# A streaming LoRA kernel on one core: a 16-tile load cut into two of 8 tiles, stores that follow, and the last wait moved to GpSimd

## The chip, the cores and the metric

The kernel runs on one core of one Trainium2 chip. The metric is the device time of one execution in microseconds (us); the time of a kernel is the median of its runs. A profile is a further execution of the same program, recorded by the hardware profiler. Its span runs from the first to the last instruction of the core; the execution's own time lies a little above its span.

## The reference, cut to what matters

```python
batch, seq, d_model, r = 16, 512, 768, 16
# x: [16, 512, 768], A: [768, 16], B: [16, 768], scale = 0.5, all float32
lora = np.matmul(np.matmul(x, A), B)
return (x + scale * lora).astype(np.float32)
```

With the two outer dimensions of x flattened there are 8192 rows of 768 numbers. Each row is read once (25.2 MB in all), gets a correction of rank 16 and is written once (another 25.2 MB).

## The kernel before

**Tiles and pieces.** The 8192 rows are 64 tiles of 128 rows. All of x stays on the chip in one buffer, `xs`, with 64 slots per partition; results are added in place and stored from the same buffer, so no load ever waits for a buffer to come free. The tiles come in seven loads, `LOADS = [2, 2, 4, 8, 16, 16, 16]` (line 13), and leave in nine stores, `STORES = [2, 2, 4, 8, 16, 8, 8, 8, 8]` (line 14). One load covers a contiguous stretch of rows of x, and each partition takes `n` consecutive rows of it (`rows`, a `"(p s) d -> p s d"` view), so a load of 16 tiles moves one run of 16 x 3072 bytes for each of 128 partitions, and a load of 8 tiles one run of 8 x 3072 bytes. A store takes a slice of the load's piece that its tiles belong to.

**Chunks.** Arithmetic goes by chunks of four tiles, 16 chunks in all (`CHUNK = 4`). For one chunk:

- VectorE (line 94, two casts) and ScalarE (line 92, one cast) narrow x to float16 in `xh`. The first cast of each engine that touches a new load waits for that load (`narrowed`).
- TensorE transposes the narrowed blocks by matmuls with an identity (line 185), ScalarE copies the transposes out of PSUM (line 135), TensorE multiplies them by A (line 193), and ScalarE copies that result, scaled, to `yt` (line 139).
- TensorE multiplies `yt` by B (line 204, one tile at a time into two PSUM buffers), and VectorE adds the product to x in place (line 146, `summed`).

**Order.** Each engine's order is written out by hand, and engines wait for each other through semaphores alone. On VectorE the casts of chunk c+1 stand between the additions of chunk c-1: cast, two additions, cast, two additions (the loop that calls `narrowed` and `summed`). So a cast that waits for a load holds up the additions behind it. TensorE works on chunk c while it expands chunk c-1. After the last addition that a store needs, VectorE drains (line 150) and raises the semaphore `added`.

**Queues.** All loads and stores are issued by SyncE (lines 81, 110, 113 and 124), in this order: two loads, A, B, the other loads but the last, a wait for `prep` (A and B have been taken out of the slots that they borrow in `xs`), the last load, and then for each store a wait on `added` and the store. Every store raises the one semaphore `stored` by 16 when it has landed. SyncE's last instruction waits until all of them have.

**GpSimd** has little to do: it zeroes the borrowed slots and builds the identity at the start (lines 98 to 101), and then runs straight to the end of the program.

Of the kernel before, what the change touches and what calls it, by code (L numbers as in the profile page):

```python
# [9 lines left out]
MM_DT = mybir.dt.float16  # L10


LOADS = [2, 2, 4, 8, 16, 16, 16]
STORES = [2, 2, 4, 8, 16, 8, 8, 8, 8]

CHUNK = 4

# [2 lines left out]
def kernel(  # L20
# [8 lines left out]
    nc = tc.nc  # L29
# [14 lines left out]
    NB = D // 32  # L44
    assert D % W == 0 and sum(LOADS) == NT == sum(STORES)
    n_splits = [(n0, min(512, D - n0)) for n0 in range(0, D, 512)]
# [16 lines left out]

    room = NT - LOADS[-1]
    a_rows = xs[0:32, room, 0 : 32 * R].rearrange("b (a r) -> b a r", r=R)
# [3 lines left out]
    def rows(t2, t0, n):  # L69
        return t2[ds(t0 * P, n * P), :].rearrange("(p s) d -> p s d", s=n)  # L70

    with tc.tile_critical():  # L72
        names = "zeroed ident a b a_t prep fed0 fed1 fed2 turned got proj y lora freed added".split()
        S = {k: nc.alloc_semaphore(name=f"s_{k}") for k in names}
        landed = [nc.alloc_semaphore(name=f"s_load{i}") for i in range(len(LOADS))]
        stored = nc.alloc_semaphore(name="s_stored")
        part_of = [i for i, n in enumerate(LOADS) for _ in range(n)]

        def load(i):
            t0, n = sum(LOADS[:i]), LOADS[i]  # L80
            nc.sync.dma_start(out=xs[:, t0 : t0 + n, :], in_=rows(x2, t0, n)).then_inc(landed[i], 16)
# [31 lines left out]
        nc.sync.dma_start(out=b_f32, in_=B).then_inc(S["b"], 16)  # L113
        for i in range(2, len(LOADS) - 1):
            load(i)
        nc.sync.wait_ge(S["prep"], 1)
        load(len(LOADS) - 1)
        done = 0
        for k, n in enumerate(STORES):
            i = part_of[done]  # L120
# [4 lines left out]
                out=rows(out2, t0, w)[:, piece, :], in_=xs[:, done : done + n, :]  # L125
            ).then_inc(stored, 16)
            done += n
        nc.sync.wait_ge(stored, 16 * len(STORES))


        narrowed(nc.scalar, 0, 2)
# [19 lines left out]

        ends = {sum(STORES[: i + 1]) for i in range(len(STORES))}
        nc.vector.sem_inc(S["freed"], 2)
# [112 lines left out]
```

## Time and profile before

| what | before |
|---|---|
| median of three runs | 128.37 us |
| the three runs | 126.47, 128.37, 132.39 us |
| the profiled execution's own time | 126.03 us |
| span of the profiled execution | 124.3 us |
| mean granted TensorE clock | 0.855 |
| bytes moved by DMA | 50.45 MB, mean 406 GB/s |
| busy: TensorE, VectorE, ScalarE, GpSimd | 93.0, 80.2, 76.7, 1.2 us |

A view that gives a table by stretches has, for each stretch of time, its length, the busy time of each engine with the number of instructions that started in it, the granted TensorE clock, the mean busy share of the 16 DMA engines and the rate in GB/s. A packet counts where it starts, so that in short stretches the share can be over 1. A view of waits says which engine and line stood idle, for whom, how long in total, how often, and the longest. In a timeline a row has its start, its length, the engine, the line, the operation and, in square brackets, the idle time before it and what ended that.

### The profile page before, as it was taken

How to read it: one execution, taken by the hardware profiler on the slowest of the kernel's cores; microseconds unless marked ns; L12 is line 12 of the kernel's file. 1: busy time of each engine (PE TensorE's matmuls, PEld its weight loads, DVE VectorE, ACT ScalarE, POOL GpSimd, SP SyncE). 2: the span in 40 equal slices, each digit the busy share in tenths (PEclk: the TensorE clock that was granted, in tenths of full speed). 3: DMA queues.
4: the chain of work that ended last, by engine and by line, in shares of the span. 5: the costliest groups of instructions: out<-in, count | busy, mean ns of one | idle time of the engine just before them, and what ended most of it. 6: DMA issues, size and time to landing. Idle time of an engine off the chain costs nothing. (4 is left out here: it accounts for less than half of the span.)

```text
span 124.3 us, 1800 instructions
## 1 busy us (share of the span) xinstructions
PE 93.0 (75%) x608; PEld 42.0 (34%) x608; DVE 80.2 (65%) x102; ACT 76.7 (62%) x129; POOL 1.2 (1%) x7
## 2 busy tenths in 40 slices
PE   0014996999259999999999999999999999750000
PEld 0012443345115335425544445444454445210000
DVE  0049208993195744655999999989999997773000
ACT  0047498688516266347989889898898988600000
POOL 3000000000000000000000000000000000000000
PEclk9999999999955555557999999999999999995555
DMA  3999999799699979969799999998989999998980
GB/s 89 406 399 435 459 522 443 316 506 475 301 491 506 443 316 506 477 301 491 309 414 443 459 435 475 475 443 348 491 348 443 435 403 467 403 451 340 388 380 8
DMA packets 2374, 50.45 MB, mean 406 GB/s; under 512 B 284, under 2 KB 284, under 8 KB 836
## 3 DMA queue, kind: packets, MB, share of 16 engines
q1 hardware_dynamic: 2372, 50.43, 95.5%
q14 instruction: 2, 0.02, 0.0%
HBM read 25.26 MB, written 25.17 MB: 406 GB/s over the span
## 5 line engine op out<-in xcount | busy, mean ns | idle before, releaser
L146 DVE TENSOR_TENSOR xs<-xs,lo_ps 128x768 f32<-128x768 f32 x64 | 58.1, 950 | 10.0 <-PE lo_ps L204 9.7
L135 ACT CAST xt<-xt_ps 128x512 f16<-128x512 f32 x96 | 52.5, 579 | 14.4 <-PE xt_ps L185 12.9
L185 PE MATMUL xt_ps<-ident,xh 128*128 128x128 f16 x384 | 37.0, 240 | 8.8 <-PEq L178 8.8
L193 PE MATMUL yt_ps<-xt,a_mm 128*16 128x512 f16 x96 | 35.8, 431 | 1.6 <-PEq L178 1.6
L94 DVE CAST xh<-xs 128x1024 f16<-128x1024 f32 x32 | 22.0, 690 | 22.6 <-DMA xs<-in_x_dram 18.0
L204 PE MATMUL lo_ps<-b_mm,yt 16*128 16x512 f16 (+1 forms) x128 | 29.9, 352 | 8.4 <-PEq L178 6.6
L185 PEld LDWEIGHTS xt_ps<-ident,xh 128*128 128x128 f16 x384 | 24.8, 107 | 29.4 <-issue 29.4
L92 ACT CAST xh<-xs 128x1024 f16<-128x1024 f32 x16 | 16.8, 1047 | 1.2 <-DMA xs<-in_x_dram 1.2
L204 PEld LDWEIGHTS lo_ps<-b_mm,yt 16*128 16x128 f16 x128 | 9.9, 96 | 20.0 <-issue 15.3
L139 ACT ACTIVATE yt<-yt_ps 16x512 f16<-16x512 f32 x16 | 9.4, 587 | 8.3 <-PE yt_ps L193 8.3
L193 PEld LDWEIGHTS yt_ps<-xt,a_mm 128*16 128x16 f16 x96 | 7.3, 89 | 20.1 <-issue 15.9
L92 ACT ACT_TABLE_LOAD x1 | 1.3, 1283 | 8.0 <-DMA xs<-in_x_dram 8.0
L158 DVE STREAM_TRANSPOSE xs<-xs 32x512 f32<-32x512 f32 x1 | 1.0, 1036 | 0.0
L162 DVE CAST a_mm<-xs 32x96 f16<-32x96 f32 x4 | 0.9, 232 | 0.1
L164 DVE CAST b_mm<-xs 16x768 f16<-16x768 f32 x1 | 0.5, 547 | 0.0
L98 POOL MEMSET xs<- 32x512 f32 x1 | 0.5, 514 | 0.5 <-SPq L72 0.5
L101 POOL TENSOR_SCALAR_AFFINE_SELECT ident<-ident 128x128 f16<-128x128 f16 x1 | 0.3, 292 | 0.2 <-POOL ident L99 0.2
L99 POOL MEMSET ident<- 128x128 f16 x1 | 0.2, 194 | 0.0
L247 POOL MEMSET const-bfloat16-1.0<- 128x1 bf16 x1 | 0.1, 102 | 0.0
L247 POOL MEMSET const-uint8-127<- 128x1 uint8 x1 | 0.1, 102 | 0.0
L247 POOL MEMSET const-float32-0.0<- 128x1 f32 x1 | 0.1, 99 | 0.2 <-issue 0.2
L247 POOL MEMSET const-float32-1.0<- 128x1 f32 x1 | 0.1, 99 | 0.0
## 6 DMA issues: line engine op xcount, KB each, us to landing
xs<-in_x_dram SPq DMA_DIRECT2D x3, 6144.0 KB, 43.7
out_dram<-xs SPq DMA_DIRECT2D x5, 3072.0 KB, 15.0
out_dram<-xs SPq DMA_DIRECT2D x1, 6144.0 KB, 20.2
xs<-in_x_dram SPq DMA_DIRECT2D x1, 3072.0 KB, 15.7
xs<-in_x_dram SPq DMA_DIRECT2D x2, 768.0 KB, 5.5
xs<-in_x_dram SPq DMA_DIRECT2D x1, 1536.0 KB, 8.9
out_dram<-xs SPq DMA_DIRECT2D x2, 768.0 KB, 42.8
out_dram<-xs SPq DMA_DIRECT2D x1, 1536.0 KB, 41.2
```

Source lines behind the costliest of these rows:

```text
L92: i = engine.copy(out=xh[u], in_=src)
L94: i = engine.tensor_copy(out=xh[u], in_=src)
L98: nc.gpsimd.memset(a_rows, 0.0).then_inc(S["zeroed"], 1)
L135: nc.scalar.copy(out=xt[j], in_=xt_ps[j % NX]).then_inc(S["got"], 1)
L139: nc.scalar.activation(out=yt, in_=yt_ps, func=mybir.ActivationFunctionType.Copy, scale=sc).then_inc(S["y"], 1)
L146: nc.vector.tensor_tensor(out=xs[:, k, :], in0=xs[:, k, :], in1=lo_ps[k % 2], op=add).then_inc(S["freed"], 1)
L158: nc.vector.transpose(out=a_t, in_=a_rows.rearrange("b a r -> b r a")).then_inc(S["a_t"], 1)
L162: nc.vector.tensor_copy(out=a_mm[ds(32 * k, 32), :, :], in_=a_tv[:, k, :, :])
L164: nc.vector.tensor_copy(out=b_mm, in_=b_f32).then_inc(S["prep"], 1)
L185: i = nc.tensor.matmul(xt_ps[j % NX][:, ds(s * P, P)], xh[u][:, s, ds(h * P, P)], ident, start=True, stop=True,)
L193: i = nc.tensor.matmul(yt_ps, a_mm[:, j, :], xt[j], start=(j == 0), stop=(j == ND - 1))
L204: i = nc.tensor.matmul(lo_ps[s % 2][:, ds(n0, w)], yt[:, ds(s * P, P)], b_mm[:, ds(n0, w)], start=True, stop=True,)
```

## The change

The load of tiles 16 to 31 becomes two loads of 8 tiles, so that there are eight loads. The store of tiles 16 to 31 becomes two stores of 8 tiles, one for each of these pieces, so that there are ten stores of at most 8 tiles. The wait for all stores moves from SyncE's queue to GpSimd's, where it comes after the building of the identity. The arithmetic and its order on TensorE, VectorE and ScalarE stay as they are; VectorE gets one more drain and semaphore, and its wait for tiles 16 to 31 becomes two waits, one for each piece.

```diff
-LOADS = [2, 2, 4, 8, 16, 16, 16]
-STORES = [2, 2, 4, 8, 16, 8, 8, 8, 8]
+LOADS = [2, 2, 4, 8, 8, 8, 16, 16]
+STORES = [2, 2, 4, 8, 8, 8, 8, 8, 8, 8]
...
             ).then_inc(stored, 16)
             done += n
-        nc.sync.wait_ge(stored, 16 * len(STORES))
+
+        nc.gpsimd.wait_ge(stored, 16 * len(STORES))
```

## The prediction, made before the changed kernel was run

> **What bounds the kernel now.** I read the page's slices first (DMA at 9 nearly throughout, the clock at 5 for a stretch in the middle and at the end), then the waits, then tables by stretches around both places, then each DMA's time to landing. The page's slices:
>
> ```profile
> PEclk9999999999955555557999999999999999995555
> DMA  3999999799699979969799999998989999998980
> ```
>
> A kernel that moves 50.45 MB with its DMA engines at work from 3 to 122 us is bound by transfers unless these run dry. They run dry once, as this table by stretches shows:
>
> ```profile
> 111.00:112.00 1.00, 0.48 (x2) 0.12 (x2) 1.00 (x3) 0.00 (x0) 0.00 (x0) 1.00 0.97 418
> 112.00:112.80 0.80, 0.00 (x0) 0.00 (x0) 0.80 (x2) 0.00 (x0) 0.00 (x0) 0.63 0.43 184
> 112.80:113.40 0.60, 0.00 (x0) 0.00 (x0) 0.12 (x1) 0.00 (x0) 0.00 (x0) 0.50 0.10 41
> 113.40:114.20 0.80, 0.00 (x0) 0.00 (x0) 0.00 (x0) 0.00 (x0) 0.00 (x0) 0.50 1.08 461
> 114.20:121.30 7.10, 0.00 (x0) 0.00 (x0) 0.00 (x0) 0.00 (x0) 0.00 (x0) 0.50 0.92 391
> 121.30:122.30 1.00, 0.00 (x0) 0.00 (x0) 0.00 (x0) 0.00 (x0) 0.00 (x0) 0.50 0.06 25
> ```
>
> The share falls to 0.43 and 0.10 while VectorE makes the last addition, that is 0.8 x 0.57 + 0.6 x 0.90 = 1.0 us lost, and recovers when the last store arrives. At the end a share of 0.06, one engine of 16, is still working 1 us after the rest. So two things end together: VectorE hands over the last store 1.0 us late for 15 DMA engines, and one DMA engine lags, never runs dry and sets the end. The landing views say how it came to lag: the last four stores, of 8 tiles each, issued at 83.1, 93.4, 103.6 and 113.0, took 17.6, 15.0, 12.1 and 10.0, so they landed at 100.7, 108.4, 115.7 and 123.0. The steps are 7.7, 7.3 and 7.3 (and 7.7 before them: the store of 72.8 took 20.2). Loads show the undisturbed pace: the loads of tiles 16 to 31 and 32 to 47 landed at 3.86 + 29.7 = 33.55 and 48.1, 14.5 for 16 tiles or 7.27 for 8. While the engines compute, the laggard loses 0.4 us per 8-tile store; when they stop, nothing.
>
> Why is VectorE so late? The waits, and the timeline at the longest of them that has a load behind it in mid-stream:
>
> ```profile
> DVE xh L94 <- DMA xs<-in_x_dram: 18.0, 3, 8.0
> DVE xs L146 <- PE lo_ps L204: 9.7, 16, 2.2
> ```
>
> ```profile
> 33.64 0.69 DVE L94 CAST xh<-xs 128x1024 f16<-128x1024 f32 x1 [4.66 <-DMA xs<-in_x_dram]
> ```
>
> The first of VectorE's three waits, 8.0, is the start; the second, 5.4 at 19.1, is for tiles 8 to 15; the third, 4.66, is for the 16-tile load, and is the one that the change touches. TensorE starves with it, and its clock goes:
>
> ```profile
> 29.00:31.80 2.80, 2.73 (x19) 1.24 (x19) 0.00 (x0) 2.36 (x5) 0.00 (x0) 1.00 0.81 351
> 31.80:35.30 3.50, 0.00 (x0) 0.00 (x0) 1.66 (x3) 1.63 (x2) 0.00 (x0) 0.77 1.04 449
> 35.30:57.60 22.30, 22.19 (x97) 8.95 (x98) 13.65 (x17) 11.30 (x20) 0.00 (x0) 0.50 0.98 424
> 57.60:112.20 54.60, 50.82 (x376) 23.68 (x374) 49.47 (x61) 44.84 (x77) 0.00 (x0) 1.00 1.01 429
> ```
>
> TensorE does nothing from 31.8 to 35.3, the clock is halved within that stretch, and for the next 22.3 us TensorE is busy 22.19 and yet shows only 97 matmuls, 4.3 a us against 376 / 54.6 = 6.9 afterwards. VectorE's first casts of chunks 4 and 8 stand at 33.64 and 62.32, 28.7 us for four chunks. From chunk 8 to chunk 15 (98.35) it is 36.0 for seven, 5.15 each. The half clock therefore cost 28.7 - 4 x 5.15 = 8.1 us of compute.
>
> **The change part by part.**
>
> *The load cut in two.* Tiles 16 to 23 land one half-load after tiles 8 to 15 (3.3 + 15.7 = 19.0, plus 7.27), at 26.3; tiles 24 to 31 at 33.6 as now. VectorE comes to the cast of chunk 4 at 33.64 - 4.66 = 28.98, 2.7 after the landing, so the 4.66 goes. What is late next: at 5.15 a chunk it wants tiles 24 to 31 (chunk 6) at 39.3, against 33.6; tiles 32 to 47 (chunk 8) at 49.6, against 48.1 and about 0.1 for the cut; tiles 48 to 63 (chunk 12) at 70.2, against 11.8 + 51.0 = 62.8. The thinnest cover is 1.4 us at chunk 8; if it is gone, VectorE waits what is missing and has room for it (below). Without the idle stretch at 31.8 the clock should stay, so chunk 15 comes at 28.98 + 11 x 5.15 = 85.6 instead of 98.35, and the last addition ends at 113.0 - 12.7 = 100.3.
>
> *The stores.* With adds two chunks behind the casts, the stores of tiles 16-23, 24-31 and so on issue near 49.5, 59.8, 70.1, 80.4, 90.7 and 100.3. The queue needs each of them when the one before has landed: 77.5 for the first (the store issued at 47.0 took 30.5), then one every 7.27: 84.8, 92.0, 99.3, 106.6 and 113.8. An engine without the lag needs them up to 1 us earlier. The cover is 12 us or more, and 4 even if the clock falls as it does now (8.1 us). So the hole of 1.0 us closes. This is worth nothing by itself, since the laggard never saw the hole. The laggard gains where compute stops 12.7 us earlier: 12.7 / 7.7 x 0.4 = 0.65 us. Bounds: nothing, if its lag comes from the stores themselves; and at most its whole distance to the others without the hole, 1.3 (122.95 against about 121.6) + 1.0 = 2.3. I take 0.65, as the two steps of 7.3 are the row nearest to it.
>
> *More transfers.* One more load and one more store. The load of tiles 8 to 15 took 19.0 - 11.7 = 7.3 from the landing before it (2.82 + 8.9), twice that is 14.6, against 14.5 for 16 tiles at once: 0.07 for a load, the same taken for a store, +0.1 in all; the low bound is 0, the high bound 0.4 (two of the steps of 7.7 against 7.3). SP issues one DMA more ahead of its wait for `prep` (0.45 us a DMA): it now waits 7.0 us there, which hides it, and the last load would otherwise start up to 0.5 later against 51.0 in the queue.
>
> The Trainium skill, "DMA: Bandwidth & Descriptors", sections "Anatomy of one DMA" and "Rules for kernel authors", speaks against the cut: a transfer has a fixed cost of about 2 us, fitted on the GpSimd path, and many small ones should be joined into a large one. By it two more transfers in a full queue would add up to 4 us; the rows above, one landing straight behind another, say 0.1.
>
> *One more drain on VectorE*, with what it stands ahead of, the next cast. The nine drains last 1.5 us in the median but overlap the addition that they wait for; even all of it lies under the 12 of cover. 0.
>
> *The last wait on GpSimd.* Behind it on GpSimd is only the end of the program; its own work ended at 2.1 us. SP, which now waits 9.6 us there, passes on and meets the others at the end barrier, all of which then wait for GpSimd. From the landing, 122.95, to the span's end lie 1.3 us. GpSimd's wait for its own memset at the start cost it 0.23, SP's waits at the barrier 0.5 to 0.7: I take 0, from -0.3 (a hop less) to +0.5 (a hop more).
>
> *Sum*, against the profiled execution: 126.03 - 0.65 + 0.1 + 0 = **125.5 us**. Bounds: 126.03 - 2.3 - 0.3 = 123.4, and 126.03 + 0.4 + 0.5 = 126.9. This execution is 2.3 below the median shown (128.37) and 0.4 below the lowest run. Why the runs spread over 126.5 to 132.4 no row shows. The profiled one has no slack at all between VectorE and the last store, so each us that the clock stays low longer goes to the end; this is my reading of the spread, and the change would take it away with 12 us of slack. So 125.5 stands for the median too, -2.2%.
>
> The trace has 22.3 us at half clock with TensorE busy for 22.19 of them. The Trainium skill, "TensorE: Matmul & The Clock Gate", section "The HAM clock gate", lets the full clock return after about 3.4 us of sustained work. By the page the half clock would have cost an estimated 1.7 us (half of 3.4) and not 8.1, so the change would bring VectorE's end forward by 4.66 + 1.7 = 6.4 only, to 106.6 instead of 100.3; by either the last store is issued ahead of the queue, and the sum is the same but for some 0.3 of the laggard's gain.
>
> **The rivals.**
>
> 1. *The spread is the transfers' own* (some runs move bytes more slowly). For it: DMA is near 9 in all slices, and the one lagging engine shows that a DMA engine can run slower. Against it: loads land at an even 7.27 per 8 tiles. The median would gain only the 0.65 - 0.1: 128.37 - 0.55 = 127.8 us, the same within 2%.
> 2. *The laggard stays as it is*, its lag belonging to the stores: 126.03 + 0.1 = 126.1, and the hole's 1.0 us shows nowhere. Within 2% of the median. For it: 0.4 a store is small and rests on four steps.
> 3. *Slower: the added transfers have a fixed price in the full queue.* Two of them, on the laggard's path. It needs 2.6 us over the median, so 1.3 us each if runs spread as before, or 2.4 each counted from the profiled execution; at 2.4 the time is 130.9. Against it: the 0.07 above. No wait takes its place, since the cover is 12.
>
> **How the numbers follow.** My forecast has 0.55 (with the time at 124.1 to 126.4, three parts in four of it under 128.37 x 0.98 = 125.8), rival 1 has 0.22, rival 2 has 0.18 and rival 3 has 0.05. About 2% is also what a measurement of this kernel can tell from no change. Faster: 0.55 x 0.75 + 0.18 x 0.4 + 0.22 x 0.1 = 0.50, the last for an uneven spread; slower 0.05; same 0.45. The range has to take in rival 1 and the low bound nearly: 123.9 to 128.0; the forecast's own is 124.1 to 126.4.
>
> **What would show it.** In the changed kernel: VectorE's waits for loads fall from 18.0 to about 13.4; the clock stays at 9 from its first rise to the last matmul; last addition near 100 us; no hole in the DMA shares before the end; the last store takes over 20 us to land instead of 10.0; steps between store landings of 7.3 from about 97 us on. I am wrong if the clock falls elsewhere, if a wait at chunk 8 of over a us appears, if landings step by over 7.7, or if the tail after the last landing is over 1.8 us.

## The result, and the profile after

| what | before | changed |
|---|---|---|
| median of 8 runs | 126.43 us | 125.27 us |
| lowest and highest run | 125.59, 132.39 us | 125.11, 125.76 us |
| ratio to before, 95% interval | | 0.9938 (0.9913 to 0.9963) |
| profiled execution's own time | 126.03 us | 125.31 us |
| span | 124.3 us | 123.5 us |

The changed kernel is 0.6% faster, about 0.8 us: clear of the measurement's uncertainty and well inside 2%. The ratio leaves out runs over 1.5% above the fastest of their kernel (two of the eight before, none of the changed).

The slices of the changed kernel's page:

```profile
PEclk9999999589999999999999999999999975555555
DMA  3999999999999699899889999999999999999990
```

The long stretch of half clock is gone, though a short one stands in the eighth slice. VectorE's waits and, from its timeline, the only wait for a load in mid-stream that is left, with the first cast of chunk 4:

```profile
DVE xh L94 <- DMA xs<-in_x_dram: 13.1, 2, 7.8
DVE xs L147 <- PE lo_ps L205: 4.8, 13, 0.9
```

```profile
18.90 0.69 DVE L94 CAST xh<-xs 128x1024 f16<-128x1024 f32 x1 [5.35 <-DMA xs<-in_x_dram]
...
30.20 0.69 DVE L94 CAST xh<-xs 128x1024 f16<-128x1024 f32 x1 [0.20 <-PE xt_ps L186]
```

The 4.66 us for the 16-tile load no longer appear; chunk 4, 33.64 before, starts at 30.20. The 5.35 for tiles 8 to 15 remain, and it is these that the short loss of clock follows, as a table by stretches has it (columns as before: after the names the clock, the DMA share, GB/s):

```profile
18.90:22.00 3.10, 2.13 (x15) 0.88 (x15) 2.97 (x4) 2.57 (x4) 0.00 (x0) 0.99 1.00 428
22.00:25.40 3.40, 3.40 (x18) 1.75 (x17) 2.57 (x4) 2.09 (x4) 0.00 (x0) 0.50 1.03 441
25.40:100.50 75.10, 70.63 (x527) 33.05 (x524) 68.95 (x85) 63.06 (x109) 0.00 (x0) 1.00 1.00 428
```

Half clock for 3.4 us instead of 23.9. The last addition ends at 101.1 instead of 112.9, and the end has no hole:

```profile
104.00:108.00 4.00, 0.00 (x0) 0.00 (x0) 0.00 (x0) 0.00 (x0) 0.00 (x0) 0.50 0.97 418
108.00:112.00 4.00, 0.00 (x0) 0.00 (x0) 0.00 (x0) 0.00 (x0) 0.00 (x0) 0.50 1.00 430
112.00:116.00 4.00, 0.00 (x0) 0.00 (x0) 0.00 (x0) 0.00 (x0) 0.00 (x0) 0.50 1.04 449
116.00:120.00 4.00, 0.00 (x0) 0.00 (x0) 0.00 (x0) 0.00 (x0) 0.00 (x0) 0.50 0.93 399
```

The share of 0.10 is nowhere now. Yet compute that ends 11.8 us earlier moved the end by only 0.72. The last store shows where they went, into the queue (the issue, then its time to landing):

```profile
L124 SPq DMA_DIRECT2D out_dram<-xs x1: 333/333/333, 101.2 to 101.2; - x1
...
DMA to landing us min/median/max: 21.3/21.3/21.3
```

It waits 21.3 us for what the earlier one waited 10.0. The last landing is at 122.50 instead of 122.97 (0.47), and the span ends 1.04 after it instead of 1.28 (0.24). Together 0.71, which is the whole change of the profiled time.

### The profile page after: what moved, and what is told of

Read it like the earlier page. It is cut to its first block, busy times and chain, and to the rows that moved or that the text cites. A ratio compares the mean times of both kernels' runs of the same rounds, so it can differ in the third digit from the quotient of the medians.

```text
span 123.5 us, 1804 instructions
## 1 busy us (share of the span) xinstructions
PE 84.3 (68%) x608; PEld 39.7 (32%) x608; DVE 80.2 (65%) x102; ACT 76.2 (62%) x129; POOL 1.1 (1%) x7
## 5 line engine op out<-in xcount | busy, mean ns | idle before, releaser
L186 PE MATMUL xt_ps<-ident,xh 128*128 128x128 f16 x384 | 34.4, 229 | 8.6 <-PEq L179 8.6
L194 PE MATMUL yt_ps<-xt,a_mm 128*16 128x512 f16 x96 | 32.9, 396 | 1.8 <-PEq L179 1.6
L94 DVE CAST xh<-xs 128x1024 f16<-128x1024 f32 x32 | 22.0, 689 | 15.3 <-DMA xs<-in_x_dram 13.1
L186 PEld LDWEIGHTS xt_ps<-ident,xh 128*128 128x128 f16 x384 | 23.0, 102 | 26.9 <-issue 26.9
L205 PE MATMUL lo_ps<-b_mm,yt 16*128 16x512 f16 (+1 forms) x128 | 26.6, 324 | 5.4 <-PEq L179 3.5
```

The lines of the kernel that those rows point to most:

```text
L94: i = engine.tensor_copy(out=xh[u], in_=src)
L186: i = nc.tensor.matmul(xt_ps[j % NX][:, ds(s * P, P)], xh[u][:, s, ds(h * P, P)], ident, start=True, stop=True,)
L194: i = nc.tensor.matmul(yt_ps, a_mm[:, j, :], xt[j], start=(j == 0), stop=(j == ND - 1))
L205: i = nc.tensor.matmul(lo_ps[s % 2][:, ds(n0, w)], yt[:, ds(s * P, P)], b_mm[:, ds(n0, w)], start=True, stop=True,)
```

## The experiments

The first four ran on one chip, the next four on another, then three and one. Each has its ratio to the kernel before on its own chip.

**One part at a time.** First GpSimd's wait alone, on the kernel before:

```diff
-        nc.sync.wait_ge(stored, 16 * len(STORES))
+        nc.gpsimd.wait_ge(stored, 16 * len(STORES))
```

> The kernel before with one edit: the wait for all stores is GpSimd's instead of SyncE's. Theory (the end of the program is one hop shorter when GpSimd waits): from the last landing to the end of the span 1.0 us as in the changed kernel, not 1.3, and the time 0.3 us below before; compute still ends near 113 us and the hole in the DMA share stays. Rival (the shorter tail comes with the other edits): tail 1.3 us, time as before. If the clock is late in coming back, the time varies by as much as before does.

Measured: 125.70 us, ratio 0.9980 (0.9957 to 1.0002). From the last landing to the end 1.04 us, as the theory had it. The interval just takes in 1, so the 0.24 us rest on the traces: 1.28 in every trace where SyncE waits, 1.02 to 1.04 in every trace where GpSimd does. Compute ended at 109.2, not near 113, and there was no hole; of this below.

The reason shows in the rows of the end barrier (instruction, count, durations in ns, first and last start). First the kernel before:

```profile
L72 SPq EVENT_SEMAPHORE  x3: 17/28/28, 123.1 to 123.4; - x3
...
L72 ACTq DRAIN  x1: 8/8/8, 123.2 to 123.2; - x1
L72 POOLq DRAIN  x1: 41/41/41, 123.2 to 123.2; - x1
```

Then the changed kernel:

```profile
L72 SPq EVENT_SEMAPHORE  x3: 17/27/28, 101.6 to 101.8; - x3
...
L72 ACTq DRAIN  x1: 8/8/8, 101.6 to 101.6; - x1
...
L72 POOLq DRAIN  x1: 41/41/41, 122.7 to 122.7; - x1
```

All engines but GpSimd go through the first step of the barrier at 101.6, while the stores are still running; after the last landing only GpSimd's drain and what follows is left. Before, all of them go through that step behind the last landing (122.97), near 123.2.

Then the pieces alone, with SyncE waiting again:

```diff
-        nc.gpsimd.wait_ge(stored, 16 * len(STORES))
+        nc.sync.wait_ge(stored, 16 * len(STORES))
```

> The changed kernel with SyncE waiting for the stores again; loads and stores in the new pieces. Theory: compute ends near 101 us, no hole in the DMA share, tail 1.3 us, time 0.3 us above the changed kernel (125.6 against 125.3), and its runs lie as close together as those of the changed kernel. Rival (most of the gain is GpSimd's wait): time as the kernel before, about 126.4.

Measured: 125.54 us, ratio 0.9974 (0.9961 to 0.9986). Compute ended at 99.6, tail 1.28. The pieces are worth about 0.33 us and GpSimd's wait about 0.24; neither is the whole.

And the store's cut alone, on the kernel before:

```diff
-STORES = [2, 2, 4, 8, 16, 8, 8, 8, 8]
+STORES = [2, 2, 4, 8, 8, 8, 8, 8, 8, 8]
```

> The kernel before with the store of tiles 16 to 31 cut in two and nothing else. Theory (the load's cut does the work, the store's does nothing): VectorE still waits 4.7 us for the 16-tile load and TensorE's clock still falls there, compute ends near 113 us, time within 0.2 us of before (126.2 to 126.6). Rival (the earlier store fills the queue better): time 0.5 us or more below before, with compute still late.

Measured: 125.96 us, ratio 1.0011 (0.9998 to 1.0024), nothing. So what the pieces gain needs the load's cut. The load's cut without the store's was not run: a store here takes a slice of one load's piece, so a 16-tile store does not fit two pieces of 8. Tables by stretches of this kernel, and then of the one with both cuts:

```profile
31.00:36.00 5.00, 1.37 (x8) 0.40 (x8) 2.58 (x4) 2.18 (x3) 0.00 (x0) 0.92 0.80 344
36.00:48.00 12.00, 12.00 (x55) 5.06 (x55) 7.20 (x10) 5.86 (x11) 0.00 (x0) 0.50 1.05 455
```

```profile
31.00:36.00 5.00, 4.86 (x39) 2.33 (x38) 4.90 (x7) 4.52 (x9) 0.00 (x0) 1.00 1.19 511
36.00:48.00 12.00, 11.71 (x88) 5.49 (x87) 11.14 (x15) 10.99 (x19) 0.00 (x0) 1.00 0.95 410
```

With the 16-tile load TensorE is idle for 3.6 of 5 us, and then needs 12 us at half clock for 55 matmuls. With the load cut it never stops and does 88.

**The price of a transfer.** The changed kernel in pieces of 4 tiles:

```diff
-LOADS = [2, 2, 4, 8, 8, 8, 16, 16]
-STORES = [2, 2, 4, 8, 8, 8, 8, 8, 8, 8]
+LOADS = [2, 2, 4, 4, 4] + [4] * 8 + [16]
+STORES = [2, 2] + [4] * 15
```

> The changed kernel with pieces of 4 tiles: LOADS 2, 2, 4, 4, 4, then eight of 4, then 16; STORES 2, 2, then fifteen of 4. That is 13 transfers more than in the changed kernel. Theory (a transfer in a full queue costs only the few ns that shorter runs cost): at 0.035 to 0.08 us each 0.5 to 1.0 us more, 125.8 to 126.3. Rival (a fixed price of 1.3 to 2.4 us for each transfer): 17 to 31 us more, 142 to 156. Compute waits less for its first loads and ends before 101 us, which by the theory gives nothing.

Measured: 125.72 us, ratio 0.9995 (0.9982 to 1.0007). Against the changed kernel's 0.9938 and 0.9959 (its second measurement, below) that is 0.5 to 0.7 us for 13 transfers, 0.04 to 0.06 us each. No fixed price of the rival's size exists in this queue.

**How much compute the end can bear.** A VectorE reduction of 128 x 640 is added behind the casts of chunks 4 to 15 (0.81 us each; its result is unused): one per chunk in the changed kernel, two per chunk, and one per chunk in the kernel before.

```diff
                     narrowed(nc.vector, c + 1, u)
+                    if c + 1 >= 4 and u < 1:
+                        nc.vector.tensor_reduce(
+                            out=spare[:, 2 * c + u, :],
+                            in_=xs[:, ds((c + 1) * CHUNK, CHUNK), ds(0, 160)],
+                            op=mybir.AluOpType.max,
+                            axis=mybir.AxisListType.X,
+                        )
```

> The changed kernel with one more VectorE reduction (128 x 640, its result unused) in each of the chunks 4 to 15, about 0.73 us each, 8.8 us in all. Theory (the changed kernel has some 12 us of slack between the last addition and the queue): the last addition ends near 110 us instead of 101, and the time stays within 0.3 us of the changed kernel, 125.3. Rival (compute still sets the end): time up by some 5 to 9 us.

Measured: 125.48 us, ratio 0.9962 (0.9946 to 0.9978): 9.7 us of work for nothing. The last addition came at 104.4, not 110: it moved by 3.3 us, so over half of the added work went into gaps that VectorE had.

> The changed kernel with two such reductions in each of the chunks 4 to 15, some 17 us in all. Theory: the slack is used up, the last addition ends near 118 us, the last store lands 8.5 to 10 us later, and the time is 129 to 131.5 us. Rival (the stores are late for another reason, compute is never the bound): time 125.3.

Measured: median 125.71 us, ratio 0.9984 (0.9956 to 1.0012), a miss: 19.5 us of work still fit in most runs, all of them with a granted clock of 0.93 or more. Single runs lie higher with a lower clock: 131.2 at 0.876, 135.7 at 0.812. The profiled one (131.65, clock 0.862) has a stay of 23.9 us at half clock, from 22.2 on, behind the wait for tiles 8 to 15. It shows what the end looks like once the slack is gone:

```profile
116.00:119.00 3.00, 1.80 (x8) 0.44 (x6) 2.64 (x3) 0.00 (x0) 0.00 (x0) 0.80 0.92 393
119.00:121.00 2.00, 0.11 (x1) 0.00 (x0) 0.99 (x2) 0.00 (x0) 0.00 (x0) 0.50 0.00 0
121.00:122.00 1.00, 0.00 (x0) 0.00 (x0) 0.00 (x0) 0.00 (x0) 0.00 (x0) 0.50 1.51 639
```

The DMA engines stand still until the last store is issued at 120.2, and it lands 8.7 us later.

> The kernel before with one such reduction in each of the chunks 4 to 15. Theory (before has no slack at its end): the last addition moves from 113 to 118 to 122 us (VectorE has idle time for some of it while TensorE's clock is low), and the time rises by about as much, to 131 to 135 us. Rival (before is bound by its transfers and has slack as the changed kernel does): time within 0.5 us of before.

Measured: 126.13 us, ratio 1.0000 (0.9979 to 1.0020), a miss that matters most: in most runs the kernel before takes the same 9.7 us without getting slower. The ratio rests on six of its ten runs; the four others took 128.0 to 134.8 us, at granted clocks of 0.80 to 0.85. The last addition in this trace is at 112.7, as late as in the profile that the prediction was read from, and the queue runs dry there too (a share of 0.20 from 112.8 to 113.4), with next to nothing lost. Without the added work it is at 109.2 and 109.4 in the two traces that keep the 16-tile load. The clock's line of the profiled kernel before has eight slices below 9 in mid-stream. Here is that of the kernel with GpSimd's wait alone, with the same loads:

```profile
PEclk9999999999955557999999999999999999655555
```

Five slices there, 13.7 us in the clock's records against 23.9. The stay at half rate differs from one execution to the next, and the one profiled before had a long one.

**Whose is the lag?** The changed kernel's transfers of x alone (arithmetic, A and B left out, so that the output is x):

> The changed kernel's loads and stores of x alone: no arithmetic, the loads of A and B are left out, and the output is x itself. Each store waits for its load only. Theory (one or two DMA engines lag because the other engines are at work): the 16 engines end within 1 us of each other and the span is 120.5 to 121.5 plus 1.0. Rival (the lag belongs to the transfers): the last engine still lands 1.5 to 2 us after the others, span 123 to 123.5. Either way this is the floor that the transfers set.

Measured: 124.55 us, ratio 0.9883 (0.9865 to 0.9902), last landing at 121.74: neither theory. Most engines end near 120.5, as ever; one is still 1.1 later, not 2. By the ratios the changed kernel is 0.7 to 1.0 us above this floor. So the lag has two parts. To separate "while compute runs" from "any compute", half of the arithmetic was left out (tiles 32 to 63 are stored as loaded):

```diff
-    NC = NT // CHUNK
+    NC = NT // CHUNK // 2
...
-            nc.sync.wait_ge(S["added"], k + 1)
+            if done < NC * CHUNK:
+                nc.sync.wait_ge(S["added"], k + 1)
+            else:
+                nc.sync.wait_ge(landed[i], 16)
```

> The changed kernel with the arithmetic of chunks 0 to 7 alone; tiles 32 to 63 are stored as they were loaded, so half of the output lacks its correction. Every load, store, A and B are as in the changed kernel. Compute ends near 60 us. Theory (one DMA engine's stores run slower while the compute engines are at work, about 0.55 us in each 10 us, and only then): next to none of the lag between 63 and 101 us is left, the time is that of the transfers alone, 124.5 to 124.8. Rival (the lag comes with the loads of A and B, or with any compute at all, not with how long it lasts): 125.2 to 125.5, as the changed kernel.

Measured: 125.01 us (124.24 to 125.37), ratio 0.9923 (0.9896 to 0.9949), between the two. The traces' packets of 24,576 bytes, 912 ns each where nothing disturbs them, tell the parts from each other. Counted are those slower than 930 ns, by the time at which they start:

```
kernel                   last addition   70 to 95 us        95 to 120 us
stores cut only             109.4        26 of 443          12 of 434
one reduction per chunk     104.4        26 of 436           7 of 435
changed                     101.1        26 of 444           4 of 433
changed, again              100.1        26 of 442           2 of 435
half of the arithmetic       58.7         0 of 441           0 of 437   (longest 912)
transfers only                 -          0 of 446           0 of 434   (longest 912)
```

The slow ones take about 965 ns. In 25 us one engine moves 25 / 0.965 = 26 of them, and in the changed kernel's trace, from 69.5 to 94.5, each starts where the one before it ends: it is one engine, all of whose stores are 5.8% slower while the compute engines are at work, and by nothing once they stop. (Where the queue had run dry and filled again, as in the kernel before at 114.7, one packet on each engine is slow too, at 935 to 955 ns.) That part of the theory holds: 0.55 us for each 10 us of compute. What the trace with half of the arithmetic has beside it is an engine that came late out of its last load, at 63.87 against 62.85 of the next. From there on it loses nothing: 64 tiles at 7.27 us per 8 are 58.2, and 63.87 + 58.2 = 122.1, where the last landing is. In the transfers alone, 63.48 + 58.2 = 121.7, again the last landing. The trace does not name the engines; that the one late at the load is the last at the end rests on these sums. The last packet of a load on an engine, where loads give way to stores, takes up to 2.8 us in the changed kernel and up to 3.6 in the transfers alone, instead of 1.82.

**Two further versions, with the changed kernel beside the first.** Finer early pieces:

```diff
-LOADS = [2, 2, 4, 8, 8, 8, 16, 16]
-STORES = [2, 2, 4, 8, 8, 8, 8, 8, 8, 8]
+LOADS = [2, 2, 4, 4, 4, 8, 8, 8, 8, 16]
+STORES = [2, 2, 4, 4, 4, 8, 8, 8, 8, 8, 8]
```

> The changed kernel with finer early pieces: LOADS 2, 2, 4, 4, 4, 8, 8, 8, 8, 16; STORES 2, 2, 4, 4, 4, then six of 8. VectorE no longer waits 5.4 us for tiles 8 to 15, so compute ends near 97 us instead of 101. Theory: 4 us less of the slower stores give 0.2 us, two more loads and one more store cost 0.1 to 0.2 us, together 125.1 to 125.3, no measurable gain on the changed kernel. Rival (an earlier end of compute is worth as much as it is early): 121 to 122.

> The changed kernel as it is, on the same chip as the two others. Theory: 125.2 to 125.5, 0.5 to 0.7 us below before, no run over 126.

Measured: 125.23 us, ratio 0.9948 (0.9935 to 0.9961), and 125.30 us, ratio 0.9959 (0.9947 to 0.9972): the intervals overlap, no gain can be told. Compute ended at 98.9 and 100.1.

Smaller pieces at the turn from loads to stores:

```diff
-LOADS = [2, 2, 4, 8, 8, 8, 16, 16]
+LOADS = [2, 2, 4, 8, 8, 8, 8, 8, 8, 8]
```

> The changed kernel with its two loads of 16 tiles cut into 8-tile pieces as well: LOADS 2, 2, 4, then seven of 8; STORES as in the changed kernel, each of them now a whole piece. The space that A and B borrow moves with the last load. In the traces the last packet of the last load on each engine, 49,152 bytes, takes 1.9 to 2.8 us instead of 1.82 where loads give way to stores, on one engine about 1 us. Theory (that loss belongs to the turn from loads to stores and not to the packet's size): the last load lands at 63.4 to 64.4 us as now, two more loads cost 0.1 us, time 125.2 to 125.5. Rival (it grows with the packet): the last load lands near 63.2 us and the time is 124.8 to 125.0, below the changed kernel.

Measured: 125.33 us, ratio 0.9961 (0.9946 to 0.9976), the last load at 63.5: the same time as the changed kernel. Cutting the last loads does not buy the loss at the turn back in time. Whether that loss grows with the packet stays open: 63.5 is the lower edge of what the theory gave and 0.3 above the rival.

## Why the prediction was right, and where it was not

- **The time.** 125.5 forecast, 125.27 measured, and 125.31 in the profiled execution, for which the sum was made. By its parts: the last landing was forecast 0.55 earlier (0.65 less 0.1 for the added transfers) and came 0.47 earlier, and the end behind it, put at 0, came 0.24 nearer. So the sum missed about 0.16 us: 0.24 that it did not have, less 0.08 that it had too much.
- **The wait.** Right: 18.0 fell to 13.1 (13.4 forecast), no wait at chunk 8, and the six later stores were issued from 50.7 to 101.2 (49.5 to 100.3 forecast).
- **The clock.** "The clock should stay" was wrong in this execution by 3.4 us, behind the wait for tiles 8 to 15 that the change leaves; "the clock falls elsewhere" was one of the signs of being wrong. The prediction showed the 4.66 us for the 16-tile load as the longest wait in mid-stream, but the one for tiles 8 to 15 was longer, 5.36. Six of the seven further traces with both cuts and all of the arithmetic show no drop at all. The seventh, with two reductions per chunk, has the long stay of 23.9 us behind that same wait, from 22.2 on, while its first reduction comes at 33.0 only; so the change does not rule it out. In the changed kernel the drop cost next to nothing, by the slack: 125.31 us against 125.25 in the second trace of it, which has none.
- **The laggard, 0.65.** Mechanism right, and the size nearly: 0.47 measured where 0.65 less the 0.1 for transfers was forecast. The rate is 0.55 us per 10 us of compute, near what was read (0.4 per 7.7, or 0.52), and 11.8 us of it would be 0.65. The rest is within what single traces differ by: the last landing is at 122.83 to 123.07 in the four traces with the 16-tile load, at 122.29 to 122.64 in six with both cuts (the queue never dry, no pieces of 4). What the prediction did not see is another engine that is late in the changed kernel. It leaves its last load at 11.6 + 52.6 = 64.2:

```profile
L81 SPq DMA_DIRECT2D xs<-in_x_dram x1: 328/328/328, 11.6 to 11.6; - x1
...
DMA to landing us min/median/max: 52.6/52.6/52.6
```

  Before it was 11.8 + 51.0 = 62.8. 64.2 + 58.2 = 122.4, so this engine now seems to end as late as the laggard (the last two landings are 122.45 and 122.50), and a further gain on the laggard alone would show next to nothing.
- **More transfers, 0.1.** Right: 0.04 to 0.06 each. The fixed cost of about 2 us in the Trainium skill ("DMA: Bandwidth & Descriptors", "Anatomy of one DMA"), fitted there on the GpSimd path, does not show for these transfers, which SyncE issues into a full queue; the measurement decides.
- **GpSimd's wait, 0.** This term was missing: 0.24 us gained, near the end of the range given for it (-0.3). I looked at the hops after the wait and not at which of them could run ahead of it.
- **The comparison with the median.** This is the step that failed, and with it the forecast of 2.2% and the chance of 0.5 for more than 2%: 0.6% was measured. "The profiled one has no slack at all" was read from one execution and does not hold for most. Others with the 16-tile load end their additions near 109.3, 3.6 us earlier, with the queue full, and bear 9.7 us of added work. So the hole of 1.0 us and the 128.37 of three runs were not typical of the kernel before; with 34 runs on another chip its median is 125.88. The reading of the spread, a clock that stays low longer, fits the record: of these 34 runs the six longest (127.1 to 131.9 us) have the six lowest granted clocks (0.802 to 0.816, all others 0.838 or more), and none of the 13 runs of the changed kernel is above 125.8. No trace of such a long run of the kernel before was kept, so this is not shown.
- **The rivals.** The first (the spread is the transfers' own) was right in that the gain is small, on a kernel that its transfers already bound in most runs. But no run shows its reason, transfers that are slower in some runs, and the clocks above speak against it. The second (the lag belongs to the stores) is refuted by the count of packets for the slow engine; the lag at the turn from loads to stores, though, is there without any compute. The third is refuted by the pieces of 4.

Open: why the last load mostly comes out later on one engine in the traces with both cuts (63.4 to 64.4) than in those with the 16-tile load (62.9 to 63.5); and what in the compute engines' work slows one DMA engine's stores. No experiment here tells its causes apart, and every trace is of a recorded execution, so the recording itself is not ruled out.

## What to carry to other kernels

Where a queue of transfers is full, an earlier end of compute turns into waiting in the queue: before pricing a removed stall, compare the time at which each store is issued with the time at which the one before it lands. One profiled execution with a long stay at half clock can look balanced between compute and transfers when most are not, so slack should be read from more than one. It can pay to put a last wait where the other engines can go through the end barrier's first step ahead of it; here that was GpSimd, worth 0.24 us, and no engine but SyncE and GpSimd was tried.

## What the runs showed of the hardware that was not expected

- Behind a wait for a load in mid-stream TensorE's clock stayed at half rate for 3.41, 13.65 or 23.89 us (by the clock's records: two, three and two stays, in six traces), although TensorE was busy for 22.19 of 22.30 us in one of the longest. The two longer times are four and seven times the shortest. The Trainium skill ("TensorE: Matmul & The Clock Gate", "The HAM clock gate") has the full clock back after at least one busy window of about 3.4 us; only the shortest of these agrees with one.
- While the compute engines work, one DMA engine of 16 is 5.8% slower in storing (26 of 444 packets in 25 us in the changed kernel, none in the two traces without compute there).
- Where loads give way to stores, the last packet of a load takes up to 2.8 us instead of 1.82 in the changed kernel, and one engine comes out about 1 us behind the next (63.87 against 62.85 with half of the arithmetic).
